# Starting every SBUF tile and pool of a decoder trunk at a multiple of 128 bytes

## The chip, the cores and the metric

The kernel runs on one core of a Trainium2 chip. The metric is the device time of one execution in microseconds (us), the median over runs. A profiled execution stands beside the timed ones; all rows shown below come from it.

## What is computed

Two layers of a causal decoder over 1,024 positions with a model width of 1,024, in float32. Cut to what matters here:

```python
for i in range(DEPTH):                       # DEPTH = 2
    hn = rmsnorm(h, attn_norm[i])
    mix = sb_rwkv_mixer(hn, ...) if i % 2 == 0 else mla_mixer(hn, positions, ...)
    h = h + mix
    h = h + conv_glu(rmsnorm(h, ffn_norm[i]), ffn_w_in[i], ...)   # FFN_DIM = 2816, causal width-3 convolution
    e = rmsnorm(p[i] @ ple_w_proj[i], ple_norm[i])
...
```

A sigmoid gate from a 1024 x 1024 product (`ple_w_gate`) scales `e` before it is added to `h`, and a last RMSNorm ends the program. The even layer's mixer is stick-breaking attention beside RWKV-7 heads; the odd layer's is latent attention (MLA) with low-rank projections.

## The kernel before

The program is one straight list of instructions per engine, with features on the 128 partitions and positions along a partition, in two blocks of 512. Nearly all of TensorE's work are projections. They are done in split form: each float32 matrix is written as a high and a low part of type float32r (`split`, lines 182 to 186, and `split_scaled`, lines 188 to 192: ScalarE makes the high part, VectorE or GpSimd the low one), and `mm3` (line 202 on, the matmul is line 211) sums three products:

```python
seq += [[(wh, xh), (wh, xl), (wl, xh)], ...][0 if part is None else 1 + part]
for i, (w, x) in enumerate(seq):
    nc.tensor.matmul(ps, lhsT=w, rhs=x, start=first and i == 0, stop=last and i == len(seq) - 1)
```

Each is a 128 x 128 weight tile, loaded as the stationary operand, against 512 moving columns. Line 211 issues 9,624 matmuls. The stages, in order:

- `hybrid_in` and `hybrid_mix`: input projection and mixer of layer 0.
- `out_proj`: 384 matmuls of the output projection (moving `xh`, `xl`, weights `whi`, `wlo`).
- `ffn_in`: 1,848 matmuls, 11 pairs x 2 x 7 products x 4 x 3. Of the seven products of a pair, two have moving operands in `mh` and `ml` (528 matmuls) and five in `x2` to `x6` (1,320; the profile writes all of them as `x`).
- `ffn_out`: 1,056 matmuls, 11 x 8 x 2 x 2 x 3, moving `mh` and `ml`; its sums are added to `h` by VectorE at line 607.
- `ple`: 480 matmuls in each layer (moving `ph`, `pl`, then `xh`, `xl`); in layer 1 the last ones are cut in half-width pieces (`CUTS`), which makes 552 instructions, 144 of them 256 columns wide.
- `mla_front` and `mla_attention`: 240 matmuls of the down projection, 312 of the up projections (moving `qn`, `kvn`) and 192 of half width (`whiv`, `wlov`), then attention.
- The odd layer then runs `out_proj`, `ffn_in`, `ffn_out`, `ple` and `final`: the same code as in layer 0.

Tiles come from pools. A pool is placed at its opening, on the left (addresses grow upwards, from behind the constants) or, with `side="right"`, from the top of a partition downwards; within a pool the tiles follow each other, each rounded up to 32 bytes. Most tiles are multiples of 2,048 bytes, so the few small ones decide where all others begin. The left side starts at byte 19,584 (a multiple of 128); the pool `row` of the tail holds two 16-byte tiles `sdt`, and what is opened behind it begins 64 bytes past a multiple. The right side starts at 229,344, which is 96 past a multiple, and so do the blocks `mh` and `ml` and, in layer 1, the weights' pool `w1`, which in layer 0 lies on the left. By these addresses, which the built program lists, the operands of line 211 stand as follows (remainder of the start address by 128 bytes):

| stage | moving | stationary | matmuls |
|---|---|---|---|
| layer 0 input projection | 96 | 96 | 1,272 |
| layer 0 `out_proj` | 64 | 0 | 384 |
| layer 0 `ffn_in`: `x` / `mh`, `ml` | 64 / 96 | 0 | 1,320 / 528 |
| layer 0 `ffn_out` | 96 | 0 | 1,056 |
| layer 0 `ple`, MLA down projection | 64 | 0 | 720 |
| MLA up projections / of half width | 96 / 0 | 0 / 96 | 312 / 192 |
| layer 1 `out_proj` | 64 | 96 | 384 |
| layer 1 `ffn_in`: `x` / `mh`, `ml` | 64 / 96 | 96 | 1,320 / 528 |
| layer 1 `ffn_out` | 96 | 96 | 1,056 |
| layer 1 `ple` | 64 | 96 | 552 |

The input projection's operands are far from each other (`xh` from byte 21,472, `whi` from 157,664).

Of the kernel before, what the change touches and what calls it, by code (L numbers as in the profile page):

```python
# [11 lines left out]
F32 = mybir.dt.float32  # L12
R = mybir.dt.float32r
I32 = mybir.dt.int32
BF = mybir.dt.bfloat16
AF = mybir.ActivationFunctionType
# [4 lines left out]
P = 128  # L21
S = 1024
D = 1024
KD = D // P
BW = 512
NBLK = S // BW
# [18 lines left out]
RAWS = 8  # L45

CUTS = (256,)
SB_COST = PAIRS * KD * (KD + 1) // 2
# [28 lines left out]

NCOLS = _col_layout()


class Banks:


    def __init__(self, places):
        self.places, self.n = places, 0

    def tile(self, shape, dtype, name):
        pool, name = self.places[self.n % len(self.places)]
        self.n += 1
        return pool.tile(shape, dtype, name=name)  # L90
# [16 lines left out]
class Trunk:  # L107
# [4 lines left out]
    def constants(self):  # L112
        nc, tc = self.nc, self.tc
        cp = self.ctx.enter_context(tc.tile_pool(reuse_waits="tile", name="const", bufs=1))
        self.cols = cp.tile([P, NCOLS], F32, name="cols")
        nc.sync.dma_start(out=self.cols, in_=self.t["cols"])
        self.ident = cp.tile([P, P], F32, name="ident")
        make_identity(nc, self.ident)
        self.ones = cp.tile([P, P], F32, name="ones")
        nc.vector.memset(self.ones, 1.0)  # L120
        self.eps = cp.tile([P, 2], F32, name="eps")
        self.scrap = cp.tile([1, 1], F32, name="scrap")
        nc.vector.memset(self.eps[:, 0:1], NORM_EPS)
        nc.vector.memset(self.eps[:, 1:2], GN_EPS)

        self.identb = cp.tile([P, P], BF, name="identb")
        nc.vector.tensor_copy(out=self.identb, in_=self.ident)

        self.causal, self.before = [cp.tile([P, P], BF, name=n) for n in ("causal", "before")]
        for m, sign, cmp in ((self.causal, 1, OP.is_ge), (self.before, -1, OP.is_gt)):  # L130
            nc.vector.memset(m, 0.0)
            nc.gpsimd.affine_select(out=m, in_=m, pattern=[[sign, P]], base=0, channel_multiplier=-sign, compare_op=cmp, fill=-1e30)
# [187 lines left out]
    def open_tail(self, ctx, wp=None):  # L320

        tc = self.tc
        self.wbufs = 3, 6, 2
        self.wp = wp or ctx.enter_context(tc.tile_pool(reuse_waits="tile", name="w", bufs=2))
        self.row = ctx.enter_context(tc.tile_pool(reuse_waits="tile", name="row", bufs=6))
        pools = [ctx.enter_context(tc.tile_pool(reuse_waits="tile", name=f"mm{i}", bufs=4, space=PSUM)) for i in range(2)]
        self.pm = Banks([(x, "mm") for x in pools for i in range(4)])

    def open_operand(self, ctx, scratch=True):

        tc = self.tc
        self.xp = ctx.enter_context(tc.tile_pool(reuse_waits="tile", name="x", bufs=NBLK))
        self.sp = ctx.enter_context(tc.tile_pool(reuse_waits="tile", name="s", bufs=2)) if scratch else None

# [96 lines left out]
    def open_raw(self, ctx):  # L431
        self.rp = ctx.enter_context(self.tc.tile_pool(reuse_waits="tile", name="raw", bufs=RAWS))

    def conv_glu(self, h, layer, c_h, c_raw):

        nc, tc, t = self.nc, self.tc, self.t
        hs = tc.dram_tile([P, KD, S], F32, name=f"hs{layer}")
        md = [tc.dram_tile([P, S], F32, name=f"md{layer}_{i}") for i in range(NFT)]
        for b in range(NBLK):
            bs = slice(b * BW, (b + 1) * BW)  # L440
            for k in range(KD):
                nc.sync.dma_start(out=hs[:, k, bs], in_=h[:, k, bs])
        with ExitStack() as ctx:
            self.ffn_in(ctx, h, layer, c_h, md)
        c_raw.close()
        pool = c_h.enter_context(tc.tile_pool(reuse_waits="tile", name=f"h2_{layer}", bufs=1, side="right"))
        h = Rows([pool.tile([P, 2, S], F32, name=f"h2_{k}") for k in range(0, KD, 2)])
        for k in range(KD):
            for b in range(NBLK):
                bs = slice(b * BW, (b + 1) * BW)  # L450
                nc.sync.dma_start(out=h[:, k, bs], in_=hs[:, k, bs])
        with ExitStack() as ctx:
            self.ffn_out(ctx, h, layer, md)
        return h
# [60 lines left out]
    def ffn_in(self, ctx, h, layer, c_h, md):  # L515
# [3 lines left out]
        w_in = t["ffn_w_in"]  # L519
        xp = ctx.enter_context(tc.tile_pool(reuse_waits="tile", name="x7", bufs=KD))  # L520

# [4 lines left out]
        c_h.close()  # L526
        ep = ctx.enter_context(tc.tile_pool(reuse_waits="tile", name="ep", bufs=1, side="right"))

# [56 lines left out]
    def ffn_out(self, ctx, h, layer, md):  # L585
        nc, tc, t = self.nc, self.tc, self.t
        wp, pm = self.wp, self.pm
        mp = ctx.enter_context(tc.tile_pool(reuse_waits="tile", name="mraw", bufs=6))
        group = 2
# [104 lines left out]
    def rope_tables(self, sp, cosb, sinb, ssgn):  # L694
# [10 lines left out]
        parts.append(float(np.float32(left)))  # L705
        half_pi = sp.tile([P, 1], F32, name="half_pi", bufs=1)
        nc.vector.memset(half_pi, float(np.pi / 2))
        for b in range(NBLK):
# [14 lines left out]
            nc.scalar.activation(out=sinb[:, bs], in_=ang, func=AF.Sin)  # L723
            nc.scalar.activation(out=cosb[:, bs], in_=k, func=AF.Sin, scale=-1.0, bias=half_pi)
            nc.vector.tensor_scalar(out=ssgn[b], in0=sinb[:, bs], scalar1=self.col("rope_sign"), scalar2=None, op0=OP.mult)

    def mla_front(self, ctx, h, close_h):
# [8 lines left out]
        close_h()  # L736
        cp = ctx.enter_context(tc.tile_pool(reuse_waits="tile", name="mla_c", bufs=1, side="right"))
        qn = [cp.tile([P, 3, S], R, name=f"qn{i}") for i in range(2)]
# [87 lines left out]
    def mla_attention(self, qn, kvn, krope, qrope):  # L826
        nc, tc, t = self.nc, self.tc, self.t
        with ExitStack() as ctx:
            pool = lambda name, bufs: ctx.enter_context(tc.tile_pool(reuse_waits="tile", name="at_" + name, bufs=bufs))
            sizes = dict(c=1, w=2, s=2, q=4, v0=1, v1=1, m=2, r=1)  # L830
# [169 lines left out]
    def hybrid(self, h, load_h, close_h, open_blocks):  # L1000
        with ExitStack() as ctx:
            self.hybrid_in(ctx.enter_context(self.tc.tile_pool(reuse_waits="tile", name="hconst", bufs=1)), h, load_h, close_h)
            open_blocks()
            o = [[self.block_tile(b) for b in range(NBLK)] for k in range(KD)]
            self.hybrid_mix(o)
        return o

    def hybrid_in(self, cp, h, load_h, close_h):

        nc, tc, t = self.nc, self.tc, self.t  # L1010
        with ExitStack() as ctx, ExitStack() as c_start:
            xp = ctx.enter_context(tc.tile_pool(reuse_waits="tile", name="hy_x", bufs=1))
            wp = ctx.enter_context(tc.tile_pool(reuse_waits="tile", name="hy_w", bufs=2))
            sp = ctx.enter_context(tc.tile_pool(reuse_waits="tile", name="hy_s", bufs=1))
            pk = ctx.enter_context(tc.tile_pool(reuse_waits="tile", name="hy_pk", bufs=1, space=PSUM))
            pm = ctx.enter_context(tc.tile_pool(reuse_waits="tile", name="hy_p", bufs=4, space=PSUM))
            pa = ctx.enter_context(tc.tile_pool(reuse_waits="tile", name="hy_pa", bufs=2, space=PSUM))
            row = ctx.enter_context(tc.tile_pool(reuse_waits="tile", name="hy_row", bufs=4))
            self.wbufs = 2, 3, 1
            xs = self.operand(xp)  # L1020
            start = c_start.enter_context(tc.tile_pool(reuse_waits="tile", name="hy_0", bufs=2, side="right"))
            lora = start.tile([P, S], F32, name="lora", bufs=1)
# [65 lines left out]
            close_h()  # L1088
            tp = ctx.enter_context(tc.tile_pool(reuse_waits="tile", name="hy_t", bufs=1, side="right"))
            c_prep = ctx.enter_context(ExitStack())  # L1090
            pp = c_prep.enter_context(tc.tile_pool(reuse_waits="tile", name="hy_pp", bufs=1, side="right"))

            side = []
# [324 lines left out]
    def hybrid_mix(self, o):  # L1418
        tc = self.tc
        with ExitStack() as ctx:  # L1420
            pool = lambda name, bufs, **space: ctx.enter_context(tc.tile_pool(reuse_waits="tile", name=name, bufs=bufs, **space))

# [249 lines left out]
    def pool_tile(self, ctx, name, side):  # L1672
        pool = ctx.enter_context(self.tc.tile_pool(reuse_waits="tile", name=name, bufs=1, side=side))
        return pool.tile([P, KD, S], F32, name=name)

    def open_blocks(self):
        self.mp = self.ctx.enter_context(self.tc.tile_pool(reuse_waits="tile", name="blocks", bufs=8, side="right"))

    def run(self):
        nc, t = self.nc, self.t  # L1680
        self.constants()

        def load(src):
# [29 lines left out]

        wp = self.ctx.enter_context(self.tc.tile_pool(reuse_waits="tile", name="w1", bufs=2, side="right"))
        c_h = self.ctx.enter_context(ExitStack())
# [118 lines left out]
```

## Time and profile before

| | |
|---|---|
| median of 3 runs | 3049.64 us (3045.56 to 3058.18) |
| the profiled execution: its time | 3055.59 us |
| its span, first to last instruction | 3053.9 us |
| TensorE (PE) busy | 2925.0 us, 96% |
| VectorE (DVE) busy | 2072.6 us, 68% |
| ScalarE (ACT) busy | 1256.2 us, 41% |
| GpSimd (POOL) busy | 1035.7 us, 34% |
| mean granted TensorE clock | 0.97 of full speed |

A matmul's duration in the profile is longer than the distance to the next one's start, because matmuls are pipelined and their ends are modelled. So a count of matmuls in a stretch in which TensorE never pauses tells the spacing, and durations of groups are compared with each other only.

### The profile page before, as it was taken

The numbers are of one execution on the slowest core, as the hardware profiler recorded it, in microseconds if no ns is written. First come the engines' busy times: TensorE is split into PE (matmuls) and PEld (weight loads), VectorE is DVE, ScalarE is ACT, GpSimd is POOL, SyncE is SP. The second block draws the span as 40 slices with busy tenths as digits, with TensorE's granted clock in tenths as the row PEclk, the third lists the DMA queues.
The fourth block names the chain that finished last, engine by engine and source line by source line (L and its number), as shares of the span: only waits on it lengthen the run. The fifth ranks groups of instructions, "written<-read, shape, count | busy, mean of one in ns | idle before, by whom it ended". The sixth has DMA issues, their size and how long they took to land. (4 is left out here: it accounts for less than half of the span.)

```text
span 3053.9 us, 40783 instructions
## 1 busy us (share of the span) xinstructions
PE 2925.0 (96%) x14542; PEld 2238.0 (73%) x14542; DVE 2072.6 (68%) x3194; ACT 1256.2 (41%) x2269; POOL 1035.7 (34%) x804
## 2 busy tenths in 40 slices
PE   8999999999699999999998899999979999999997
PEld 6777777677488888788886656556758888888876
DVE  7766647773786676544698677776387777755577
ACT  6424436671343333311544434343243333422274
POOL 4332421112454444444323500011244444454323
PEclk9999989999799999999999899999979999999998
DMA  4344565644022222532122300013212222252111
GB/s 140 115 143 134 162 199 129 159 108 162 28 83 83 83 83 71 192 96 83 49 82 58 113 18 23 19 39 109 75 42 83 83 83 80 93 176 93 59 56 59
DMA packets 221019, 286.09 MB, mean 94 GB/s; under 512 B 62256, under 2 KB 106800, under 8 KB 220816
## 3 DMA queue, kind: packets, MB, share of 16 engines
q1 hardware_dynamic: 215632, 272.99, 29.3%
q10 hardware_dynamic: 5184, 10.49, 0.9%
q8 instruction: 115, 1.88, 0.3%
q14 instruction: 88, 0.72, 0.1%
HBM read 200.50 MB, written 81.79 MB: 92 GB/s over the span
## 5 line engine op out<-in xcount | busy, mean ns | idle before, releaser
L211 PE MATMUL mm<-x,whi 128*128 128x512 f32 x1760 | 566.9, 402 | 21.4 <-DVE x L186 12.2
L186 POOL TENSOR_TENSOR wlo<-wraw,whi 128x512 fp32r<-128x512 f32 (+2 forms) x238 | 318.6, 1346 | 558.0 <-ACT whi L185 500.8
L211 PE MATMUL mm<-mh,whi 128*128 128x512 f32 x1056 | 416.2, 395 | 6.4 <-DVE h L607 3.4
L211 PE MATMUL mm<-ml,whi 128*128 128x512 f32 x1056 | 417.7, 396 | 3.9 <-DVE ml L186 3.9
L211 PEld LDWEIGHTS mm<-x,whi 128*128 128x128 f32 x1760 | 335.2, 191 | 115.4 <-DVE x L186 20.2
L211 PE MATMUL mm<-mh,wlo 128*128 128x512 f32 x1056 | 417.1, 395 | 0.0
L211 PE MATMUL mm<-xh,whi 128*128 128x512 f32 (+1 forms) x1016 | 405.2, 399 | 7.2 <-ACT xh L191 7.2
L211 PE MATMUL mm<-xh,wlo 128*128 128x512 f32 (+1 forms) x1016 | 398.9, 393 | 1.2 <-POOL wlo L186 1.2
L607 DVE TENSOR_TENSOR h<-h,mm 128x512 f32<-128x512 f32 x352 | 241.4, 687 | 228.0 <-PE mm L211 207.7
L211 PE MATMUL mm<-xl,whi 128*128 128x512 f32 (+1 forms) x1016 | 393.1, 394 | 0.5 <-DVE xl L192 0.5
L211 PE MATMUL mm<-x,wlo 128*128 128x512 f32 x880 | 349.4, 397 | 0.0
L185 ACT CAST whi<-raw 128x512 fp32r<-128x512 f32 x264 | 163.4, 620 | 371.7 <-PE mm L211 332.5
L185 ACT CAST whi<-wraw 128x512 fp32r<-128x512 f32 (+2 forms) x242 | 142.9, 595 | 342.0 <-PE mm L211 172.7
L186 POOL TENSOR_TENSOR wlo<-raw,whi 128x512 fp32r<-128x512 f32 x104 | 158.2, 1521 | 368.8 <-ACT whi L185 368.5
L211 PEld LDWEIGHTS mm<-mh,whi 128*128 128x128 f32 x1056 | 200.0, 189 | 55.8 <-ACT mh L185 5.9
L211 PEld LDWEIGHTS mm<-ml,whi 128*128 128x128 f32 x1056 | 199.9, 189 | 51.3 <-DVE ml L186 5.6
L211 PEld LDWEIGHTS mm<-xh,whi 128*128 128x128 f32 x1016 | 194.5, 191 | 53.6 <-ACT xh L191 8.0
L211 PEld LDWEIGHTS mm<-mh,wlo 128*128 128x128 f32 x1056 | 199.8, 189 | 44.1
L211 PEld LDWEIGHTS mm<-xl,whi 128*128 128x128 f32 x1016 | 194.0, 191 | 46.0 <-issue 4.6
L211 PEld LDWEIGHTS mm<-xh,wlo 128*128 128x128 f32 x1016 | 194.1, 191 | 43.7 <-POOL wlo L186 2.1
L211 PEld LDWEIGHTS mm<-x,wlo 128*128 128x128 f32 x880 | 167.9, 191 | 38.1
L934 ACT ACTIVATE w<-s 128x512 f32<-128x512 f32 (+1 forms) x192 | 94.0, 491 | 166.8 <-PE s L932 147.5
(408 smaller groups left out, 5261.1 us busy)
## 6 DMA issues: line engine op xcount, KB each, us to landing
raw<-in_ffn_w_in SPq DMA_DIRECT2D x176, 256.0 KB
wraw<-in_ffn_w_out SPq DMA_DIRECT2D x88, 256.0 KB
md<-u SPq DMA_DIRECT2D x88, 256.0 KB
mraw<-md SPq DMA_DIRECT2D x88, 256.0 KB
wraw<-in_hyb_w_in SPq DMA_DIRECT2D x52, 256.0 KB
hs<-h SPq DMA_DIRECT2D x32, 256.0 KB
h<-hs SPq DMA_DIRECT2D x32, 256.0 KB
wraw<-in_ple_w_gate SPq DMA_DIRECT2D x32, 256.0 KB
```

What stands on the lines that cost most here:

```text
L185: nc.scalar.copy(out=hi, in_=src)
L186: (eng or nc.gpsimd).tensor_tensor(out=lo, in0=src, in1=hi, op=OP.subtract)
L211: nc.tensor.matmul(ps, lhsT=w, rhs=x, start=first and i == 0, stop=last and i == len(seq) - 1)
L607: nc.vector.tensor_tensor(out=h[:, f, bs], in0=h[:, f, bs], in1=ps, op=OP.add)
L934: nc.scalar.activation(out=w[:, :n], in_=s[:, :n], func=AF.Exp, scale=MLA_SCALE)
```

## The change

Every SBUF pool is wrapped in a class that rounds a tile's row up to 128 bytes. The constant for pi/2 moves from a tile of its own into a third column of `eps`. A pool `end` of 24 floats is opened first on the right, so that the right side begins at 229,248, a multiple of 128. The left side then begins at 19,840, also a multiple. In the built program every tile except the framework's own four small constants begins at a multiple of 128; of the 9,624 matmuls of line 211, 8,352 have both operands 128 past a multiple of 256, 1,104 have both at one, and 168 have one of each.

```diff
+END = 24
...
+class Lines:
+    def __init__(self, pool):
+        self.pool = pool
+    def tile(self, shape, dtype, **kw):
+        n, per = int(np.prod(shape[1:])), 64 if dtype is BF else 32
+        if n % per == 0:
+            return self.pool.tile(shape, dtype, **kw)
+        x = self.pool.tile([shape[0], -(-n // per) * per], dtype, **kw)[:, :n]
+        return x if len(shape) == 2 else x.rearrange("p (a b) -> p a b", b=shape[2])
...
-        self.eps = cp.tile([P, 2], F32, name="eps")
+        self.eps = cp.tile([P, 3], F32, name="eps")
...
+        nc.vector.memset(self.eps[:, 2:3], float(np.pi / 2))
...
-        self.row = ctx.enter_context(tc.tile_pool(reuse_waits="tile", name="row", bufs=6))
+        self.row = Lines(ctx.enter_context(tc.tile_pool(reuse_waits="tile", name="row", bufs=6)))
...
-        half_pi = sp.tile([P, 1], F32, name="half_pi", bufs=1)
-        nc.vector.memset(half_pi, float(np.pi / 2))
...
-            nc.scalar.activation(out=cosb[:, bs], in_=k, func=AF.Sin, scale=-1.0, bias=half_pi)
+            nc.scalar.activation(out=cosb[:, bs], in_=k, func=AF.Sin, scale=-1.0, bias=self.eps[:, 2:3])
...
         self.constants()
+        end = self.ctx.enter_context(self.tc.tile_pool(reuse_waits="tile", name="end", bufs=1, side="right"))
+        end.tile([P, END], F32, name="end")
```

All other SBUF pools are wrapped in the same way as `row`; PSUM pools are not.

The order of instructions is the same on every engine but for one VectorE instruction, and no shape changes. At the program's start VectorE's rows before were:

```order
L120 MEMSET ones 128x128
L123 MEMSET eps 128x1
L124 MEMSET eps 128x1
L131 MEMSET causal 128x64
L131 MEMSET before 128x64
```

and now they are:

```order
L136 MEMSET ones 128x128
L139 MEMSET eps 128x1
L140 MEMSET eps 128x1
L141 MEMSET eps 128x1
L148 MEMSET causal 128x64
L148 MEMSET before 128x64
```

The third `eps` row is the constant that was written later before (line 707, in the middle of layer 0's `ffn_in`).

New addresses also change which earlier tiles a tile overlaps, and a few waits are attached to other instructions of the same list. VectorE's low parts of layer 0's `out_proj`, with the semaphores that each waits for (`DMAHW` are those of loads), stood before as:

```order
L186 TENSOR_TENSOR xl<-mh,xh 128x512 [waits DMAHW3_49,DMAHW5_49,DMAHW2_49,Activation_49]
L186 TENSOR_TENSOR xl<-mh,xh 128x512 [waits Activation_49]
L186 TENSOR_TENSOR xl<-mh,xh 128x512 [waits Activation_49] x6
L186 TENSOR_TENSOR xl<-ml,xh 128x512 [waits Activation_49] x8
```

and stand now as:

```order
L203 TENSOR_TENSOR xl<-mh,xh 128x512 [waits DMAHW5_49,DMAHW3_49,Activation_49]
L203 TENSOR_TENSOR xl<-mh,xh 128x512 [waits Activation_49]
L203 TENSOR_TENSOR xl<-mh,xh 128x512 [waits Activation_49] x6
L203 TENSOR_TENSOR xl<-ml,xh 128x512 [waits DMAHW5_49,DMAHW2_49,Activation_49]
L203 TENSOR_TENSOR xl<-ml,xh 128x512 [waits Activation_49] x7
```

One wait for loads of the mixer's `xbd` tiles moved from the first low part to the ninth.

## Rows read from the trace of the kernel before

**Rows 1.** The profile's page: TensorE's share of the span, and its granted clock.
```profile
PE 2925.0 (96%) x14542; PEld 2238.0 (73%) x14542; DVE 2072.6 (68%) x3194; ACT 1256.2 (41%) x2269; POOL 1035.7 (34%) x804
...
PEclk9999989999799999999999899999979999999998
```

**Rows 2.** The chain that ended last: start us, us, what, three of its pieces.
```profile
2106.20 89.58 PE mm L211 x383
2255.33 416.53 PE mm L211 x1789
2680.86 267.98 PE mm L211 x1176
```

**Rows 3.** `ffn_out`, layers 0 and 1: length, busy PE, PEld, DVE, ACT, POOL, clock, DMA.
```profile
1280.00:1490.00 210.00, 210.00 (x902) 168.94 (x901) 109.59 (x160) 47.86 (x83) 89.57 (x73) 1.00 0.26 81
2690.00:2900.00 210.00, 210.00 (x928) 173.93 (x928) 110.35 (x162) 50.41 (x88) 98.97 (x80) 1.00 0.28 89
```

**Rows 4.** TensorE's groups, 1280 to 1490 us (`ffn_out`, layer 0): busy us, mean ns.
```profile
L211 PE MATMUL mm<-mh,wlo 128*128 128x512 f32 x301 | 120.1, 399 | 0.0
L211 PE MATMUL mm<-ml,whi 128*128 128x512 f32 x301 | 118.6, 394 | 0.0
L211 PE MATMUL mm<-mh,whi 128*128 128x512 f32 x300 | 117.6, 392 | 0.0
```

**Rows 5.** The same groups, 2690 to 2900 us (`ffn_out`, layer 1).
```profile
L211 PE MATMUL mm<-mh,whi 128*128 128x512 f32 x310 | 120.6, 389 | 0.0
L211 PE MATMUL mm<-ml,whi 128*128 128x512 f32 x309 | 120.2, 389 | 0.0
```

**Rows 6.** Groups of TensorE by shape, 850 to 1262 us (`ffn_in`, layer 0).
```profile
L211 PE MATMUL mm<-x,whi 128*128 128x512 f32 x826 | 257.3, 393 | 0.0
L211 PE MATMUL mm<-x,wlo 128*128 128x512 f32 x414 | 160.9, 389 | 0.0
```

**Rows 7.** The same groups, 2270 to 2640 us (`ffn_in`, layer 1).
```profile
L211 PE MATMUL mm<-x,whi 128*128 128x512 f32 x762 | 239.6, 396 | 0.0
L211 PE MATMUL mm<-x,wlo 128*128 128x512 f32 x381 | 150.7, 395 | 0.0
```

**Rows 8.** Groups of TensorE by shape, 348 to 378 us (input projection, layer 0).
```profile
L211 PE MATMUL mm<-xl,whi 128*128 128x512 f32 x45 | 17.5, 389 | 0.0
L211 PE MATMUL mm<-xh,wlo 128*128 128x512 f32 x45 | 17.5, 389 | 0.0
```

**Rows 9.** Groups of GpSimd and ScalarE by shape, 1280 to 1490 us.
```profile
L186 POOL TENSOR_TENSOR wlo<-wraw,whi 128x512 fp32r<-128x512 f32 x34 | 43.7, 1298 | 38.9 <-PE mm L211 38.9
...
L185 ACT CAST whi<-wraw 128x512 fp32r<-128x512 f32 x34 | 20.9, 618 | 72.7 <-issue 72.0
```

**Rows 10.** The same groups, 2690 to 2900 us.
```profile
L186 POOL TENSOR_TENSOR wlo<-wraw,whi 128x512 fp32r<-128x512 f32 x36 | 46.3, 1296 | 36.0 <-ACT whi L185 36.0
...
L185 ACT CAST whi<-wraw 128x512 fp32r<-128x512 f32 x36 | 22.2, 618 | 69.8 <-issue 69.4
```

**Rows 11.** A group of the page: VectorE's sums of `ffn_out`.
```profile
L607 DVE TENSOR_TENSOR h<-h,mm 128x512 f32<-128x512 f32 x352 | 241.4, 687 | 228.0 <-PE mm L211 207.7
```

**Rows 12.** A stretch of `ple` in layer 1: us, then busy PE, PEld, DVE, ACT, POOL.
```profile
2960.00:3010.00 50.00, 50.00 (x221) 40.00 (x220) 47.14 (x61) 26.12 (x41) 14.98 (x8) 1.00 0.09 28
```

**Rows 13.** The constant's memset: duration min/median/max, first and last start.
```profile
L707 DVE MEMSET half_pi<- x1: 59/59/59, 1246.4 to 1246.4; 128x1 f32 x1
```

**Rows 14.** In order of time: SyncE's last `xbd` load, VectorE's first low parts of `out_proj`.
```profile
634.30 0.61 SPq L1499 DMA_DIRECT2D xbd<-xt  x1
...
684.49 2.98 DVE L186 TENSOR_TENSOR xl<-mh,xh 128x512 fp32r<-128x512 f32 x2
...
698.29 1.88 DVE L186 TENSOR_TENSOR xl<-ml,xh 128x512 fp32r<-128x512 f32 x3
```

More of the change, by code (lines that the diff above doesn't have):

```diff
@@ L113, in constants @@
         nc, tc = self.nc, self.tc
-        cp = self.ctx.enter_context(tc.tile_pool(reuse_waits="tile", name="const", bufs=1))
+        cp = Lines(self.ctx.enter_context(tc.tile_pool(reuse_waits="tile", name="const", bufs=1)))
         self.cols = cp.tile([P, NCOLS], F32, name="cols")
@@ L323, in open_tail @@
         self.wbufs = 3, 6, 2
-        self.wp = wp or ctx.enter_context(tc.tile_pool(reuse_waits="tile", name="w", bufs=2))
-        self.row = ctx.enter_context(tc.tile_pool(reuse_waits="tile", name="row", bufs=6))
+        self.wp = wp or Lines(ctx.enter_context(tc.tile_pool(reuse_waits="tile", name="w", bufs=2)))
+        self.row = Lines(ctx.enter_context(tc.tile_pool(reuse_waits="tile", name="row", bufs=6)))
         pools = [ctx.enter_context(tc.tile_pool(reuse_waits="tile", name=f"mm{i}", bufs=4, space=PSUM)) for i in range(2)]
@@ L331, in open_operand @@
         tc = self.tc
-        self.xp = ctx.enter_context(tc.tile_pool(reuse_waits="tile", name="x", bufs=NBLK))
-        self.sp = ctx.enter_context(tc.tile_pool(reuse_waits="tile", name="s", bufs=2)) if scratch else None
+        self.xp = Lines(ctx.enter_context(tc.tile_pool(reuse_waits="tile", name="x", bufs=NBLK)))
+        self.sp = Lines(ctx.enter_context(tc.tile_pool(reuse_waits="tile", name="s", bufs=2))) if scratch else None
     def block_tile(self, i, dtype=F32):
@@ L431, in open_raw @@
     def open_raw(self, ctx):
-        self.rp = ctx.enter_context(self.tc.tile_pool(reuse_waits="tile", name="raw", bufs=RAWS))
+        self.rp = Lines(ctx.enter_context(self.tc.tile_pool(reuse_waits="tile", name="raw", bufs=RAWS)))
     def conv_glu(self, h, layer, c_h, c_raw):
@@ L445, in conv_glu @@
         c_raw.close()
-        pool = c_h.enter_context(tc.tile_pool(reuse_waits="tile", name=f"h2_{layer}", bufs=1, side="right"))
+        pool = Lines(c_h.enter_context(tc.tile_pool(reuse_waits="tile", name=f"h2_{layer}", bufs=1, side="right")))
         h = Rows([pool.tile([P, 2, S], F32, name=f"h2_{k}") for k in range(0, KD, 2)])
@@ L519, in ffn_in @@
         w_in = t["ffn_w_in"]
-        xp = ctx.enter_context(tc.tile_pool(reuse_waits="tile", name="x7", bufs=KD))
+        xp = Lines(ctx.enter_context(tc.tile_pool(reuse_waits="tile", name="x7", bufs=KD)))
         def weights(tiles, late=nc.vector):
@@ L526, in ffn_in @@
         c_h.close()
-        ep = ctx.enter_context(tc.tile_pool(reuse_waits="tile", name="ep", bufs=1, side="right"))
+        ep = Lines(ctx.enter_context(tc.tile_pool(reuse_waits="tile", name="ep", bufs=1, side="right")))
         def pair(i):
@@ L587, in ffn_out @@
         wp, pm = self.wp, self.pm
-        mp = ctx.enter_context(tc.tile_pool(reuse_waits="tile", name="mraw", bufs=6))
+        mp = Lines(ctx.enter_context(tc.tile_pool(reuse_waits="tile", name="mraw", bufs=6)))
         group = 2
@@ L736, in mla_front @@
         close_h()
-        cp = ctx.enter_context(tc.tile_pool(reuse_waits="tile", name="mla_c", bufs=1, side="right"))
+        cp = Lines(ctx.enter_context(tc.tile_pool(reuse_waits="tile", name="mla_c", bufs=1, side="right")))
         qn = [cp.tile([P, 3, S], R, name=f"qn{i}") for i in range(2)]
@@ L828, in mla_attention @@
         with ExitStack() as ctx:
-            pool = lambda name, bufs: ctx.enter_context(tc.tile_pool(reuse_waits="tile", name="at_" + name, bufs=bufs))
+            pool = lambda name, bufs: Lines(ctx.enter_context(tc.tile_pool(reuse_waits="tile", name="at_" + name, bufs=bufs)))
             sizes = dict(c=1, w=2, s=2, q=4, v0=1, v1=1, m=2, r=1)
@@ L1001, in hybrid @@
         with ExitStack() as ctx:
-            self.hybrid_in(ctx.enter_context(self.tc.tile_pool(reuse_waits="tile", name="hconst", bufs=1)), h, load_h, close_h)
+            self.hybrid_in(Lines(ctx.enter_context(self.tc.tile_pool(reuse_waits="tile", name="hconst", bufs=1))), h, load_h, close_h)
             open_blocks()
@@ L1011, in hybrid_in @@
         with ExitStack() as ctx, ExitStack() as c_start:
-            xp = ctx.enter_context(tc.tile_pool(reuse_waits="tile", name="hy_x", bufs=1))
-            wp = ctx.enter_context(tc.tile_pool(reuse_waits="tile", name="hy_w", bufs=2))
-            sp = ctx.enter_context(tc.tile_pool(reuse_waits="tile", name="hy_s", bufs=1))
+            xp = Lines(ctx.enter_context(tc.tile_pool(reuse_waits="tile", name="hy_x", bufs=1)))
+            wp = Lines(ctx.enter_context(tc.tile_pool(reuse_waits="tile", name="hy_w", bufs=2)))
+            sp = Lines(ctx.enter_context(tc.tile_pool(reuse_waits="tile", name="hy_s", bufs=1)))
             pk = ctx.enter_context(tc.tile_pool(reuse_waits="tile", name="hy_pk", bufs=1, space=PSUM))
@@ L1017, in hybrid_in @@
             pa = ctx.enter_context(tc.tile_pool(reuse_waits="tile", name="hy_pa", bufs=2, space=PSUM))
-            row = ctx.enter_context(tc.tile_pool(reuse_waits="tile", name="hy_row", bufs=4))
+            row = Lines(ctx.enter_context(tc.tile_pool(reuse_waits="tile", name="hy_row", bufs=4)))
             self.wbufs = 2, 3, 1
             xs = self.operand(xp)
-            start = c_start.enter_context(tc.tile_pool(reuse_waits="tile", name="hy_0", bufs=2, side="right"))
+            start = Lines(c_start.enter_context(tc.tile_pool(reuse_waits="tile", name="hy_0", bufs=2, side="right")))
             lora = start.tile([P, S], F32, name="lora", bufs=1)
@@ L1088, in hybrid_in @@
             close_h()
-            tp = ctx.enter_context(tc.tile_pool(reuse_waits="tile", name="hy_t", bufs=1, side="right"))
+            tp = Lines(ctx.enter_context(tc.tile_pool(reuse_waits="tile", name="hy_t", bufs=1, side="right")))
             c_prep = ctx.enter_context(ExitStack())
-            pp = c_prep.enter_context(tc.tile_pool(reuse_waits="tile", name="hy_pp", bufs=1, side="right"))
+            pp = Lines(c_prep.enter_context(tc.tile_pool(reuse_waits="tile", name="hy_pp", bufs=1, side="right")))
             side = []
@@ L1420, in hybrid_mix @@
         with ExitStack() as ctx:
-            pool = lambda name, bufs, **space: ctx.enter_context(tc.tile_pool(reuse_waits="tile", name=name, bufs=bufs, **space))
+            pool = lambda name, bufs, **space: (lambda x: x if space else Lines(x))(ctx.enter_context(tc.tile_pool(reuse_waits="tile", name=name, bufs=bufs, **space)))
             sizes = dict(rw=2, sw=2, ss=4, rs=2, sv=2, rz=1, sk=2, sq=3, sh=3, rp=1, ro=1)
@@ L1672, in pool_tile @@
     def pool_tile(self, ctx, name, side):
-        pool = ctx.enter_context(self.tc.tile_pool(reuse_waits="tile", name=name, bufs=1, side=side))
+        pool = Lines(ctx.enter_context(self.tc.tile_pool(reuse_waits="tile", name=name, bufs=1, side=side)))
         return pool.tile([P, KD, S], F32, name=name)
     def open_blocks(self):
-        self.mp = self.ctx.enter_context(self.tc.tile_pool(reuse_waits="tile", name="blocks", bufs=8, side="right"))
+        self.mp = Lines(self.ctx.enter_context(self.tc.tile_pool(reuse_waits="tile", name="blocks", bufs=8, side="right")))
     def run(self):
@@ L1712, in run @@
             o = self.mla_attention(*front)
-        wp = self.ctx.enter_context(self.tc.tile_pool(reuse_waits="tile", name="w1", bufs=2, side="right"))
+        wp = Lines(self.ctx.enter_context(self.tc.tile_pool(reuse_waits="tile", name="w1", bufs=2, side="right")))
         c_h = self.ctx.enter_context(ExitStack())
```

## The prediction

> **What bounds the kernel now.** Start with the page's engine table: TensorE is busy for 2925.0 us of the span, 96%, the next engine for 68% [rows 1]. The reader is to see that no other engine can set the end except at a few places. The chain of waits confirms it: in order of time its longest pieces are unbroken runs of line 211, 1,789 matmuls in 416.53 us and 1,176 in 267.98 us [rows 2]. In such a run the time is the number of matmuls times their spacing, so a change of spacing goes straight into the total. The change alters neither number nor shape of any matmul; the only thing it can change there is the spacing. The two runs already differ in it: 416.53 / 1,789 = 232.8 ns, 267.98 / 1,176 = 227.9 ns, and layer 1's `out_proj` has 89.58 / 383 = 233.9 ns. Why?
>
> The next view is the table of stretches. `ffn_out` runs the same code in both layers, and in two stretches of 210 us TensorE never pauses and has its full clock [rows 3]; full is 2.4 GHz. In layer 0 it starts 902 matmuls, in layer 1 928: 232.8 and 226.3 ns. The groups say the same: 399, 394 and 392 ns in layer 0, mean 395.0 [rows 4], and 389 in layer 1 [rows 5]. That is 6.0 ns by the durations, 6.5 by the counts. What differs is the placement: by the table of remainders the weights start at 0 in layer 0 and at 96 in layer 1, the moving operands at 96 in both. `ffn_in` is the opposite experiment. Its `x` products stand at 64 against 0 in layer 0, mean (826 x 393 + 414 x 389) / 1,240 = 391.7 ns [rows 6], and at 64 against 96 in layer 1, mean 395.7 ns [rows 7]. The same move of the weights that makes `ffn_out` faster makes `ffn_in` slower. So no remainder is good or bad by itself; the fast case is that of equal remainders. The input projection, 96 against 96, has the same 389 ns [rows 8].
>
> I read three classes from this, by the difference of the two remainders: none, 389 ns; 64 bytes, 2.7 ns more (391.7 - 389); 32 or 96 bytes, 6.0 to 6.7 ns more, for which I take 6.5, the count of the long stretch. After the change every pair of operands differs by a multiple of 128.
>
> **The change part by part.** *Tiles at multiples of 128.* Matmuls by the code, times the price:
>
> - Layer 0 `out_proj`: 384 x 2.7 ns = 1.0 us.
> - Layer 0 `ffn_in`: 1,320 x 2.7 + 528 x 6.5 = 7.0 us.
> - Layer 0 `ffn_out`: 1,056 x 6.5 = 6.9 us.
> - `ple` of layer 0 and down projection: 720 x 2.7 = 1.9 us.
> - MLA up projections: 312 x 6.5 = 2.0 us, and 192 of half width at half the price, an estimate, 0.6 us.
> - Layer 1 `out_proj`: 384 x 6.5 = 2.5 us.
> - Layer 1 `ffn_in`: 1,320 x 6.5 = 8.6 us; its other 528 are equal already.
> - Layer 1 `ple`: 408 x 6.5 + 144 x 3.25 = 3.1 us.
> - Input projection and layer 1 `ffn_out`: equal already, 0.
>
> The sum is 33.6 us. The attention's own float32r matmuls (lines 928, 931 and 932, 192 of each, at 64 against 0) would give at most 576 x 2.7 ns = 1.6 us; they stand among waits and narrower tiles, so I take 0 and keep 1.6 for the range.
>
> *Does the rest of the machine follow?* Where TensorE gets faster by 2 to 3%, its producers must too. In layer 1's `ffn_out` they already feed it at 226.3 ns, with VectorE busy for 110.35 of 210 us and GpSimd for 98.97 [rows 3], so layer 0's will. The narrow place is layer 1's `ple`, where VectorE is busy for 47.14 of 50 us [rows 12]; a gain of 3% would need 48.6 of 50. If VectorE ends last there and in layer 0's `ple`, the terms 1.9 and 3.1 are lost. I leave them in, because TensorE has no pause in that stretch, and keep the 5.0 us for the range.
>
> *The other engines and the transfers.* The same operation on the same shape, with weights at 0 and at 96: GpSimd 1298 and 1296 ns, ScalarE 618 and 618 [rows 9, 10]; I price placement at 0 there. VectorE's sums at line 607 take 687 ns [rows 11] with operands at 96 in both layers, so their row cannot tell, but they follow TensorE and have slack. Transfers: at weights' remainder 0 the DMA engines are 0.26 busy for 81 GB/s, at 96 they are 0.28 busy for 89 GB/s [rows 3], per byte the same to the rounding of two digits; 0.
>
> *The constant and the moved waits.* The memset took 59 ns and stood in the middle of `ffn_in` on VectorE, which is not the bound there [rows 13]; it now costs about as much at the start, beside the first loads. 0. The wait for `xbd` loads now stands before the ninth low part of `out_proj`; the last such load was issued at 634.30, and the first low part starts at 684.49, the ninth at 698.29 [rows 14]. The loads are over 50 us old, nothing behind it on VectorE is held up. 0.
>
> *The sum.* The profiled execution took 3055.59 us, so 3055.6 - 33.6 = 3022.0 us for one like it. It lies 6.0 us above the median of the runs shown, 3049.64; from the median the forecast is **3016 us**, 1.1% less. Bounds of the terms: 33.6 + 1.6 = 35.2 and 33.6 - 5.0 = 28.6, that is 3014 to 3021.
>
> A rule of the Trainium skill speaks against all this. Rows 3 show the same code at two spacings, 232.8 and 226.3 ns, with nothing else in the way of TensorE. The page "SBUF — State Buffer", section "Who interferes with whom", says that TensorE has two independent read ports, one for the moving operand and one for the weights, and that "PE and ACT never wait on anyone". By that, an operand's place should cost TensorE nothing and the sum would be 0; the rows disagree, since something that is no other engine slows it, but they don't show what. As a rival it stands below.
>
> **The rivals.**
>
> *Slower: zero is the worst place.* No clean stretch of line 211 shows both operands at 0, so the equal class might be special to 96. If both at 0 cost as much as the worst class, the 2,856 matmuls that are fast now would lose 2,856 x 6.5 = 18.6 us, and the 2,424 at 64 against 0 would lose 2,424 x 3.8 = 9.2 us: 3049.6 + 27.8 = 3077 us. It decides as soon as absolute remainders, not differences, count. Against it: the two layers' opposite signs in `ffn_in` and `ffn_out`, where a remainder of 0 for the weights is once the better and once the worse. Chance 0.03.
>
> *Half-way: both at 0 cost what 64 against 0 cost.* Then the fast ones lose 2,856 x 2.7 = 7.7 us, the slow ones gain 3.8 ns: 528 + 1,056 + 312 + 384 + 1,320 + 408 = 4,008 matmuls, 15.2 us. Result 3049.6 - 7.5 = 3042 us. Chance 0.05.
>
> *Placement is not the cause.* The layers also differ in where the weights' pool lies: on the left in layer 0, on the right in layer 1, and `mh` lies on the right in both, `x` on the left. "Same side fast, other side slow" fits `ffn_out` and the sign of `ffn_in`. Then aligning does nothing: 3050 us. Against it: in the input projection, `xh` and `whi` start 136,192 bytes apart and run at 389 ns [rows 8], and `x` of layer 0, on its weights' side, is still 2.7 ns slow. This is also what the change gives if the rule quoted above held. Chance 0.05.
>
> *The gain comes back as waits.* If the faster TensorE waits for VectorE or the weights' split through half of `ffn_in` too, about half of it goes: 3049.6 - 16.8 = 3033 us. For it speaks only the narrow place in [rows 12]; against it layer 1's `ffn_out`. Chance 0.05.
>
> **How the numbers follow.** The forecast has 0.82, the rivals 0.03, 0.05, 0.05 and 0.05. The likeliest case reaches from 3014 to 3021; the median of three runs can lie off by what the runs before show, from 4.1 us below their median to 8.5 above. That gives 3010 to 3030; taking in the case of returned waits, the range is 3009 to 3033 us. A measurement of this kernel tells about 0.5% from no change, 15 us: faster than 3034 is the forecast and the returned waits, of which half may fall within noise, 0.85; the half-way case, the case without effect and the rest of the waits are "same", 0.12; slower 0.03.
>
> **What would show it.** In the new profile: 389 ns for every full-width group of line 211 in `ffn_in`, `ffn_out` and `ple`, wherever TensorE doesn't pause; 928 matmuls in 210 us of either `ffn_out`; about 417 us less 8.6 for layer 1's `ffn_in`; the first layer's `ffn_in` shorter by 7. GpSimd's and ScalarE's durations stay. Wrong would be: 392 to 395 ns in layer 0's `x` products (half-way), 395 in the input projection (zero is bad), unchanged differences between the layers (another cause), or 389 ns with new pauses of TensorE that VectorE ends (returned waits).

## The result, and the profile after

The kernel before had a median of 3058.18 us in this comparison (3045.56 to 3068.93, 5 runs), the changed kernel 3023.04 us (3019.57 to 3030.21, 5 runs). The medians lie 35 us apart; the ratio, taken over the executions of both kernels, is 0.9899, with a 95% interval of 0.9875 to 0.9923. That is about 31 us, and the text below goes by it. The profiled execution took 3029.6 us; its span, 3027.9 us, is 26.0 us shorter than that of before.

The page of the changed kernel first. TensorE has the same 14,542 matmuls, and the busy times of the other engines lie within 0.6% of those of before:

```profile
span 3027.9 us, 40783 instructions
PE 2899.6 (96%) x14542; PEld 2241.8 (74%) x14542; DVE 2064.3 (68%) x3194; ACT 1256.0 (41%) x2269; POOL 1041.7 (34%) x804
```

TensorE is busy for 25.4 us less [rows 1], which is the whole gain of this execution but for 0.6 us. Two long stretches at full clock show where. Line 211 is now line 228. Stretches of the changed kernel: length, then busy PE, PEld, DVE, ACT, POOL with their instructions, clock, DMA share, GB/s. The first is `ffn_out` of layer 0, the second of layer 1, the third a stretch at the start of layer 1's `ffn_in` that speaks for the clock below, the last the tail.

```profile
1270.00:1480.00 210.00, 210.00 (x928) 173.91 (x927) 114.44 (x168) 49.87 (x86) 92.02 (x75) 1.00 0.27 84
2660.00:2870.00 210.00, 210.00 (x928) 173.87 (x927) 109.92 (x161) 47.39 (x83) 97.44 (x78) 1.00 0.31 97
2172.00:2272.00 100.00, 77.52 (x264) 54.84 (x264) 81.36 (x111) 43.27 (x71) 43.33 (x26) 0.78 0.15 48
2976.00:3028.00 52.00, 29.42 (x184) 26.83 (x182) 33.75 (x55) 23.69 (x48) 17.80 (x16) 0.79 0.23 82
```

Layer 0's `ffn_out` starts 928 matmuls in 210 us where it started 902 [rows 3]; layer 1's has the 928 that it had. The groups of TensorE say the same of one matmul. They are from four stretches: `ffn_out` of layer 0 [rows 4], `ffn_in` of layer 0 [rows 6] and of layer 1 [rows 7], and MLA's up projections.

```profile
L228 PE MATMUL mm<-ml,whi 128*128 128x512 f32 x310 | 120.6, 389 | 0.0
...
L228 PE MATMUL mm<-x,whi 128*128 128x512 f32 x821 | 252.7, 389 | 0.0
...
L228 PE MATMUL mm<-x,whi 128*128 128x512 f32 x785 | 241.6, 389 | 0.0
...
L228 PE MATMUL mm<-qn,whiq 128*128 128x512 f32 x12 | 3.7, 390 | 0.0
L228 PE MATMUL mm<-whiv,kvn 128*128 128x256 f32 x32 | 6.0, 286 | 0.0
```

Every full-width group of `ffn_in` and `ffn_out` stands at 389 ns in both layers, in layer 0's `ffn_out` down from 399, 394 and 392; the group of the up projections has 390. The half-width group of the last line has 286 ns, as it had before. The chain of the changed kernel, from three parts of the span (start us, us, what):

```profile
1662.80 6.89 PE mm L228 x29
1669.72 1.57 POOL qn L203 x2
1671.29 2.85 POOL wlo L203 x2
1674.14 2.51 POOL ml L203 x2
...
2090.80 87.09 PE mm L228 x383
2243.02 403.39 PE mm L228 x1779
2655.21 266.86 PE mm L228 x1176
...
2979.37 0.70 DVE h L666
2980.09 0.64 ACT sq L163
2980.76 0.69 DVE facc L164
...
3003.81 5.33 PE mm L228 x24
```

Against [rows 2], layer 1's `out_proj` takes 2.49 us less, and the piece of `ffn_in` runs at 403.39 / 1,779 = 226.8 ns instead of 232.8. The third piece starts 25.65 us earlier than before. At the end the gain is 26.0 us, so `ffn_out`, `ple` and the tail of layer 1 together brought 0.3 us. Three pieces of the chain of before, at the places of the first lines above and of the last four, show what changed there:

```profile
1677.39 18.03 PE mm L211 x77
...
2969.06 43.47 PE mm L211 x204
...
3030.73 4.47 PE mm L211 x24
```

At the first two places the chain ran on TensorE; now it goes by GpSimd at the one, and by VectorE and ScalarE at the other. At the third the same 24 matmuls take 0.9 us longer than before, because they now lie wholly in a stretch at the lower clock (2998.9 to 3009.1 us, granted 0.5 of full speed); before, that stretch ended at 3034.0 us, in the midst of them.

### The profile page after: what moved, and what is told of

Read it like the earlier page. It is cut to its first block, busy times and chain, and to the rows that moved or that the text cites. A ratio compares the mean times of both kernels' runs of the same rounds, so it can differ in the third digit from the quotient of the medians.

```text
span 3027.9 us, 40783 instructions
## 1 busy us (share of the span) xinstructions
PE 2899.6 (96%) x14542; PEld 2241.8 (74%) x14542; DVE 2064.3 (68%) x3194; ACT 1256.0 (41%) x2269; POOL 1041.7 (34%) x804
## 5 line engine op out<-in xcount | busy, mean ns | idle before, releaser
L228 PE MATMUL mm<-x,whi 128*128 128x512 f32 x1760 | 559.2, 398 | 19.2 <-DVE x L203 9.9
```

## The experiments

Two theories were to be told apart at first. Mine: the spacing depends on the difference of the two operands' remainders. The rival: a multiple of 128 is a good place by itself. Later the question was by which number the remainders are to be taken. Streams of 64 matmuls measured the price apart from the kernel; then pools were moved in the real one.

### Streams of matmuls at chosen places

```diff
+        for i in range(count):
+            at, wat = r // size + i % 4 * BW, w // size + i % 4 * P
+            nc.tensor.matmul(ps[:, :cols], lhsT=wt[:, wat:wat + P], rhs=x[:, at:at + cols], start=i == 0, stop=i == count - 1)
```

> Streams of 64 unbroken matmuls, each stream with its own byte offsets of the moving tile (x) and the weights (w) past a multiple of 256; nothing of the decoder is computed. Theory (only the difference of the two remainders by 128 counts): float32r with 512 columns has the fast spacing, 226.7 ns, wherever x and w are equal by 128 (0/0, 32/32, 64/64, 96/96, 128/0, 256/0, 0/128, 64/192), about 229 at a difference of 64, and about 233 at 32 and 96, on either sign. Rival 'absolute remainders': 0/0 is slower than 96/96, and 32/32, 64/64, 96/96 differ among each other. Rival 'place is not the cause': 226.7 in all streams. Open, no forecast from the theory: differences of 4, 8, 16, 48 and 112 bytes, narrower matmuls, bf16 and float32.

Both tiles begin at the same remainder by 256, so the difference of the two numbers in a name (`x`: bytes to the moving operand, `w`: to the weights) is what counts; `r` is float32r, `b` bf16, `f` float32. Groups of TensorE in that kernel: busy us, mean ns, idle.

```profile
L132 PE MATMUL r512x96w96s<-xr,wr 128*128 128x512 f32 x64 | 14.7, 389 | 0.0
L132 PE MATMUL r512x256w0s<-xr,wr 128*128 128x512 f32 x64 | 14.7, 389 | 0.0
L132 PE MATMUL r512x64w0s<-xr,wr 128*128 128x512 f32 x64 | 14.8, 392 | 0.0
L132 PE MATMUL r512x0w64s<-xr,wr 128*128 128x512 f32 x64 | 15.1, 396 | 0.0
L132 PE MATMUL r512x32w0s<-xr,wr 128*128 128x512 f32 x64 | 15.1, 395 | 0.0
L132 PE MATMUL r512x128w0s<-xr,wr 128*128 128x512 f32 x64 | 15.1, 395 | 0.0
L132 PE MATMUL r512x16w16s<-xr,wr 128*128 128x512 f32 x64 | 15.1, 396 | 0.0
L132 PE MATMUL b512x32w0s<-xb,wb 128*128 128x512 bf16 x64 | 14.0, 379 | 0.0
L132 PE MATMUL r256x0w0s<-xr,wr 128*128 128x256 f32 x64 | 7.8, 283 | 0.0
L132 PE MATMUL r256x64w0s<-xr,wr 128*128 128x256 f32 x64 | 7.7, 279 | 0.0
```

The spacing is the busy time less one duration, over 63: 227 ns in the first two lines, 229 in the third, 233 in the next four. Three things follow. The price is that of the difference, as the prediction had it: 96 against 96 is fast, 32 against 0 is slow, 64 against 0 lies between. But the period is 256 bytes and not 128: 256 against 0 is fast, 128 against 0 is slow, and so is 64 against 192. And +64 is not -64: the moving operand 64 ahead of the weights costs about 2.4 ns, 64 behind them about 6.6. Equality is not all either, since 16 against 16 is slow. The theory put on record with this run is thereby refuted in its "by 128": it had 128 against 0, 0 against 128 and 64 against 192 among the fast ones. bf16 has 379 ns and float32 has 592 ns (the float32 matmul shows as two instructions) at 0, 32, 64 and 96 alike. The last two lines are matmuls of 256 columns, where the order is another.

### More places, and streams of two places in turn

```diff
+            at, wat = (r0, r1)[i % 2] // 4 + i % 4 * BW, (w0, w1)[i % 2] // 4 + i % 4 * P
```

> More streams of unbroken matmuls alone; nothing of the decoder is computed. After the first set of streams the theory is: the spacing of full-width float32r is 226.7 ns only if both operands stand at multiples of 32 bytes and are equal by 256 (not by 128). Then 128/128, 96/96-like pairs with w + 64 (160/96, 224/160, 96/32: a difference of +64) have 229, 48/48 and 8/8 about 233 as 16/16, and 32/128, 128/32, 144/0, 176/0, 208/0, 240/0 about 230 to 235. Rival 'by 128': refuted already by 128/0. Pairs: the weights of the next matmul are loaded while this one streams. If a matmul's spacing hangs on its own weights' place, streams that alternate x = w = 0 and x = w = 128 stay at 226.7, and those that alternate x = 0, w = 128 and x = 128, w = 0 are at 233; if it hangs on the next one's weights, it is the other way round; the same for 32 and 64. Bf16: 215.8 at any difference.

Groups of TensorE of this kernel; `pair` streams change between two places of each operand at every matmul:

```profile
L133 PE MATMUL r512x128w128s<-xr,wr 128*128 128x512 f32 x64 | 14.7, 390 | 0.0
L133 PE MATMUL r512x160w96s<-xr,wr 128*128 128x512 f32 x64 | 14.8, 391 | 0.0
L133 PE MATMUL r512x32w64s<-xr,wr 128*128 128x512 f32 x64 | 15.1, 395 | 0.0
L133 PE MATMUL r512x8w8s<-xr,wr 128*128 128x512 f32 x64 | 15.1, 395 | 0.0
L145 PE MATMUL pairx0x128w0w128s<-xr,wr 128*128 128x512 f32 x64 | 14.8, 391 | 0.0
L145 PE MATMUL pairx0x128w128w0s<-xr,wr 128*128 128x512 f32 x64 | 14.9, 392 | 0.0
```

The classes hold: 128 against 128 is fast, 160 against 96 (+64) lies between, 32 against 64 (-32) and 8 against 8 are slow. One place came out otherwise than expected: 48 against 48 has 231.0 ns from start to start, not 233. Nor is bf16 quite free of its place: at 8 bytes it has 217.7 ns, at 128 215.8. The pairs were to show whether a matmul's own weights count or those loaded during it. By the starts in the trace the stream whose own places are equal has 228.6 ns, the one whose next places are equal 230.0, where a clean answer would be 227 for one and 233 for the other. With places of 0 and 32 they have 231.7 and 233.3 ns, with 0 and 64 both have 231.5 to 231.7. That question stays open; what it does show is that equal places of a matmul's own operands are not enough for 227 ns when the place changes from one matmul to the next. The prices above are those of streams, and stages, that stay at one pair of places for many matmuls.

### Everything 32 bytes further

```diff
-END = 24
+END = 16
+        self.ctx.enter_context(self.tc.tile_pool(reuse_waits="tile", name="start", bufs=1)).tile([P, 8], F32, name="start")
```

> The changed kernel with everything moved by 32 bytes on both sides: no tile begins at a multiple of 128 any more, all operand pairs still have equal remainders. Theory: the same as the changed kernel, ratio to the kernel before 0.990 (0.987 to 0.993), 389 ns in every full-width group. Rival 'a multiple of 128 is what counts' (transfers, other engines or TensorE read aligned lines faster): the gain is gone, ratio 1.000, or over it. Rival 'place is not the cause': 0.990 too, but then the next two runs stay there as well.

Measured: 3027.74 us (3020.89 to 3037.71), ratio 0.9903 [0.9873, 0.9933], and 389 ns in all groups of both `ffn_in` and `ffn_out`; one of them, from layer 0's `ffn_out`:

```profile
L229 PE MATMUL mm<-mh,whi 128*128 128x512 f32 x310 | 120.6, 389 | 0.0
```

No tile of the kernel's pools stands at a multiple of 128 any more, and the gain is all there. The multiple of 128 by itself is worth nothing that these runs can tell.

### The right side moved against the left, by 64 and by 32

```diff
-END = 24
+END = 8
```

> The changed kernel with the right side's start moved by 64 bytes: every tile still begins at a multiple of 64, and 4,512 matmuls (336 of them half as wide) have one operand on each side, 64 bytes apart. Theory: these cost 2.7 ns more each (391.7 instead of 389 in the groups), 4,176 x 2.7 + 336 x 1.35 = 11.7 us more than the changed kernel, ratio to before 0.994 (0.990 to 0.997). Rivals 'side of the memory' and 'place is not the cause': as the changed kernel, 0.990.

Measured: 3039.06 us (3034.29 to 3047.14), ratio 0.9944 [0.9921, 0.9967]: the time expected, by another composition. By the addresses 2,064 of the 4,512 matmuls stand at +64, and 2,112 with the 336 of half width at -64. By the streams' prices that is 2,064 x 2.4 + 2,112 x 6.6 = 18.9 us over the change without the half-width ones; 0.9944 - 0.9899 is 14 us. Its groups in layer 0's `ffn_out` (`m` on the right, weights on the left), and in layer 1's `ffn_in` (`x` on the left, weights on the right):

```profile
L228 PE MATMUL mm<-mh,wlo 128*128 128x512 f32 x299 | 117.8, 394 | 0.0
L228 PE MATMUL mm<-ml,whi 128*128 128x512 f32 x299 | 117.2, 392 | 0.0
L228 PE MATMUL mm<-mh,whi 128*128 128x512 f32 x298 | 115.6, 388 | 0.0
...
L228 PE MATMUL mm<-x,whi 128*128 128x512 f32 x762 | 239.0, 394 | 0.0
```

The three groups of the one direction have 391.3 ns in the mean, 2.3 over the change, the other direction 394, 5 over it. By the starts: in a long stretch of the one 920 matmuls begin in 210 us (228.3 ns), and the trace has 233.3 ns between the starts of the other. So the real kernel has the two signs of the streams as well.

```diff
-END = 24
+END = 16
```

> The same with 32 bytes: 4,512 matmuls with operands 32 or 96 bytes apart. Theory: 6.5 ns more each, 4,176 x 6.5 + 336 x 3.25 = 28.2 us more than the changed kernel, ratio to before 0.999 (0.996 to 1.002), and 395 ns in both layers' cross-side groups (first ffn_out, second ffn_in's x products), 389 in the others. Rivals as in the run before: 0.990.

Measured: 3046.18 us (3033.47 to 3052.20, 10 runs), ratio 0.9972 [0.9956, 0.9987]. The groups in the same two places:

```profile
L228 PE MATMUL mm<-mh,wlo 128*128 128x512 f32 x301 | 118.9, 395 | 0.0
...
L228 PE MATMUL mm<-x,whi 128*128 128x512 f32 x761 | 239.4, 396 | 0.0
```

Every pair across the two sides is slow, and most of the gain is gone, with the code of the changed kernel otherwise as it was.

### Every tile at a multiple of 128, the sides 128 apart

```diff
-        self.eps = cp.tile([P, 3], F32, name="eps")
-        self.scrap = cp.tile([1, 1], F32, name="scrap")
+        self.eps = cp.tile([P, 4], F32, name="eps")
+        self.scrap = self.eps[0:1, 3:4]
```

This puts two small constants into one tile, so the left side moves down by 128 bytes. What the change is called still holds of every tile, and the left is at 0 by 256, the right at 128.

> The changed kernel with 128 bytes less on the left (the one-element scrap tile becomes a column of eps): every tile still begins at a multiple of 128, no instruction moves, but 4,344 matmuls (336 of half width) have operands 128 bytes apart by 256. Theory 'equal by 256': these cost 6.5 ns more, 4,008 x 6.5 + 336 x 3 = 27 us more than the changed kernel, ratio to before 0.999 (0.996 to 1.002); 395 ns in the first ffn_out and in the second ffn_in's x products. My prediction's rule 'equal by 128', and any reason by which starting at a multiple of 128 is itself the gain: as the changed kernel, ratio 0.990, 389 ns everywhere.

Measured: 3044.06 us (3030.53 to 3060.18, 12 runs), ratio 0.9955 [0.9934, 0.9977]. Groups of TensorE: `ffn_out` of layer 0 (across the sides), then `x` in layer 0 (one side) and in layer 1 (across):

```profile
L228 PE MATMUL mm<-mh,wlo 128*128 128x512 f32 x301 | 118.9, 395 | 0.0
...
L228 PE MATMUL mm<-x,whi 128*128 128x512 f32 x815 | 251.2, 389 | 0.0
...
L228 PE MATMUL mm<-x,whi 128*128 128x512 f32 x763 | 240.8, 396 | 0.2 <-DVE x L203 0.2
```

By the rule of the prediction, remainders by 128, this kernel should have had the time of the change, 0.990. It is slower than that (its interval doesn't meet that of the change), and the groups stand as the table by 256 says. The size is less than I had expected of the table: the lower bound of what I gave was 0.996, the measured ratio is 0.9955. Across the sides stand 1,056 + 528 + 384 + 1,320 + 408 + 312 = 4,008 full-width matmuls by the tables ahead of the prediction; at 6.6 ns that is 26.5 us over the change, where 0.9955 - 0.9899 is 17 us of 3058 and the run with 32 bytes has 22. The single matmul has its full price: in the long runs of both cross-side stages the trace has 233.3 ns from start to start, against 226.7 in the change. The two intervals taken together allow 3 to 31 us, so the size can't be held against the price; the executions of this kernel range from 3030.53 us (granted clock 0.971) to 3060.18 (0.964). Where the missing part lies was not separated.

### Only the pool at the end, with the kernel before

```diff
+END = 24
...
+        end = self.ctx.enter_context(self.tc.tile_pool(reuse_waits="tile", name="end", bufs=1, side="right"))
+        end.tile([P, END], F32, name="end")
```

No tile is rounded up and no constant moved; the right side goes down by 96 bytes.

> The kernel before with nothing but the 96-byte pool at the right's top: the small tiles stay unpadded, the left stays at 64 past a multiple behind the row pool. By 256 the x products and the 64/96 ones come to +64, the mh and ml ones to 0. Theory: both ffn_out at 389 ns, x products of both layers at 391.7; 4,680 matmuls at +2.4 ns, 11 us more than the changed kernel, ratio to before 0.9935 (0.991 to 0.996). Rival 'all tiles must be aligned (transfers, other engines)': ratio near 1.000.

Measured: 3033.76 us (3023.12 to 3040.17, 6 runs), ratio 0.9923 [0.9896, 0.9950]. Layer 0's `ffn_out` and its `x` products in `ffn_in`:

```profile
L212 PE MATMUL mm<-mh,whi 128*128 128x512 f32 x310 | 120.6, 389 | 0.0
...
L212 PE MATMUL mm<-x,whi 128*128 128x512 f32 x824 | 255.6, 391 | 0.0
```

The pool alone brings 23.5 of the change's 31 us: `ffn_out` of both layers is fast, and the `x` products of both are at +64, the cheap sign. The intervals of the two ratios overlap, so the times don't show that the rounding of all tiles adds to it; the groups do, with 391 ns for the `x` products here and 389 in the change.

One more kernel was not tried: tiles rounded to 256 bytes do not fit into SBUF. By the table it would have little left to win: in the changed kernel 168 of the 9,624 matmuls differ by 128, all of them in layer 0 before its `out_proj`, 168 x 6.6 ns = 1.1 us.

## Why the prediction was right, and where it was not

The forecast of 3016 us is 7 us below the median, inside the range of 3009 to 3033, and the sign and the size come from the mechanism that the prediction named. Against one and the same execution it forecast 3022.0 / 3055.6 = 0.989, and 0.9899 [0.9875, 0.9923] was measured. From the median of this comparison, 3058.18 us, the same sum gives 3024.6. The profiled execution shows less, 26.0 us against the sum of 33.6; MLA's term and waits that came back, which the sum had at nothing, are the larger part of the difference. By its steps:

**Spacing, not other work.** Right. TensorE's busy time carries the gain, the instructions and their number are the same, and moving a pool by 32 bytes takes most of the gain away and moving all of them takes none.

**The classes.** The step "by the difference of the two remainders" was right, and "after the change every pair of operands differs by a multiple of 128" is not what makes them fast. The streams show a period of 256 bytes (128 against 0: 395 ns; 256 against 0: 389), and two prices for 64 bytes by the sign (392 and 396). The prediction could not see either: of pairs 64 bytes apart its rows show those at +64 alone. By the streams' prices, without the half-width matmuls, the change is worth 2,424 x 2.4 + 4,008 x 6.6 - 168 x 6.6 = 31.2 us, so the wrong period hardly touched the sum. That the change falls into the fast class nearly everywhere is because 9,456 of the 9,624 pairs agree by 256 as well, and that is luck: nothing in the prediction's rule asked for it. Had the two small constants shared one tile, as in the run above, the text of the change would be as true and its gain about 14 us instead of 31.

**The terms.** Compared by the starts of the same matmuls in the two profiled executions, stage by stage, in us:

| part | forecast | shorter by |
|---|---|---|
| layer 0 up to `out_proj` | 0 | 0.4 |
| layer 0 `out_proj` | 1.0 | 0.8 |
| layer 0 `ffn_in` | 7.0 | 6.5 |
| layer 0 `ffn_out` | 6.9 | 6.3 |
| layer 0 `ple`, MLA down projection | 1.9 | 0.6 |
| MLA up projections and attention | 2.6 | 0.7 |
| layer 1 `out_proj` | 2.5 | 2.5 |
| layer 1 `ffn_in` | 8.6 | 8.6 |
| layer 1 `ffn_out` | 0 | -0.8 |
| layer 1 `ple` | 3.1 | 2.6 |
| tail | 0 | -2.2 |

Where TensorE runs unbroken, the terms came true. MLA's term was too high: the half-width matmuls cost 286 ns as before, and where the full-width ones got faster, the chain goes by GpSimd's splitting (`qn`, `wlo`, `ml`) where it went by TensorE. The half price for half the width, an estimate, was wrong: streams of 256 columns have 283 ns at 0 against 0 and 279 at 64 against 0, so there the equal place is not even the best.

**Returned waits.** This rival did not come true in `ffn_in`, where it was priced, but at the stages' borders a small one did. Here are TensorE's waits for VectorE at a norm in MLA's front and, as the second line of each kernel, at the heads of the two `ffn_out` (us in total, times, longest; first before, then after):

```profile
PE mm L153 <- DVE row L147: 7.8, 1, 7.8
PE mm L211 <- DVE h L607: 3.4, 2, 1.9
...
PE mm L170 <- DVE row L164: 8.6, 1, 8.6
PE mm L228 <- DVE h L624: 5.1, 2, 2.7
```

The three waits are 0.8 to 0.9 us longer each, 2.5 us in all; that is what both `ffn_out` lack in the table, and most of what layer 0's `ple` lacks. At the heads of `ffn_out` VectorE's first sum waits in turn for the transfer `h<-hs`, for 10.8 and 10.5 us instead of 10.3 and 9.4: the transfer did not come earlier by as much as TensorE did. Another wait, that of `ffn_in` for VectorE's `x`, fell from 12.2 to 9.9 us, at the start of layer 1's `ffn_in`, where TensorE itself was slower at the lower clock (the third stretch above).

**The tail.** The prediction named layer 1's `ple` as the narrow place, VectorE busy for 47.14 of 50 us [rows 12], and kept up to 5.0 us for the range but 0 in the sum. About 2 us were lost there: a gain of 28.2 us within `ple` is one of 26.0 at the end. Of these, 1.3 us go where TensorE now waits for VectorE and the chain runs through `h`, `sq` and `facc`, and 0.7, by the starts, in the 24 matmuls at the lower clock. This was a reading of the traces; no run took work off VectorE there.

**The clock.** Not in the sum. Each of the two profiled executions has 17 stretches at the lower clock (1.2 GHz), 183.7 us of the span before and 196.2 after. An estimate from these: at half the clock a microsecond loses at most half a microsecond, so the 12.5 us can hide up to 6 us of the gain between these two executions. In the third stretch above the clock is 0.78; the same part of before shows 0.81. I have no run that shows the change to be the cause.

**The rivals.** "Zero is the worst place" and "half-way" fell with the change itself, since its groups have 389 ns. "Placement is not the cause" fell with the runs that move one side. The rule that was weighed, "PE and ACT never wait on anyone" (the Trainium skill, page "SBUF — State Buffer", section "Who interferes with whom"), is not itself refuted: in the streams no other engine works on the operands, so TensorE waits for none. What falls, for float32r, is what the prediction drew from it and from the two independent read ports, that an operand's place costs nothing: the spacing is 227 or 233 ns by the place alone. Why the place counts was not found.

**The other engines.** As forecast: GpSimd's `wlo`, ScalarE and VectorE's sums have their old durations, and neither the constant nor the moved wait shows in the long pieces of the chain.

## What to carry to other kernels

In a kernel that TensorE bounds with float32r matmuls, compare the mean duration of the same shape between stages that run the same code; a difference of a few ns that no wait explains is a reason to look at the addresses. What has to agree, in matmuls of 512 columns that keep one pair of places, is the moving operand with its weights, modulo 256 bytes and at multiples of 32, and a spare tile of some bytes at one end of a memory side can be enough. Look at the borders of such a stretch too: here 2.5 us of the gain stayed in three waits there. Before rounding every tile, measure the price with a stream of some 64 matmuls, at more remainders than the kernel happens to use: the rule read from three classes was right for this kernel and wrong as a rule.

## What was not expected of the hardware

- The price depends on the sign: moving operand 64 bytes ahead of the weights 392 ns, behind them 396.
- Equal places that are not multiples of 32 are slower: 16 against 16 has 396 ns, 8 against 8 has 395, 48 against 48 has 393.
- At multiples of 32 it was seen with float32r alone: bf16 has 379 ns at 0, 32, 64 and 96, with starts 215.8 to 216.0 ns apart (217.7 at 8 bytes), and float32 592. The Trainium skill, page "TensorE: Matmul & The Clock Gate", section "Step-by-step: what each phase is for", has 215.7 ns between matmuls of 512 columns, with which the bf16 streams agree; float32r at its best place has 226.7 ns.
- Width counts: at 384 columns 0 against 64 and 128 against 0 have 338 ns, the others tried 335 or 336; at 256 columns the groups lie between 279 and 283 ns without the order of the full width, and at 128 columns they are 274 or 275 ns everywhere.
